# A one-layer neighbourhood-attention encoder in fp32: all second-half query, key and gate units by seven products, half of the second values inside attention, row groups in turn

## The chip, the core and the metric

The kernel runs on one core of one Trainium2 chip, as one launch. The metric is the device time of that launch in microseconds (us). Engines are named as in the profile: PE is the matrix engine (PEld its weight loads), DVE the vector engine, ACT the scalar engine, POOL the GpSimd engine, and SP the engine that issues nearly all DMAs.

## The reference

One layer on x of 2048 tokens by 1024 channels, 16 heads of 64 channels, tokens on a grid of 32 rows by 64 columns:

```python
h = rmsnorm(x, g)                       # over 1024 channels
q, k, v, gate = jnp.split(h @ w_in, 4, axis=-1)      # w_in: 1024 x 4096
# each query sees 8 rows x 16 columns of keys, plus a learned bias by relative position
s = einsum(q, k) / 8 + bias             # masked outside the neighbourhood
o = einsum(softmax(s), v)
x = x + (o * silu(gate)) @ w_out
out = rmsnorm(x, norm_f)
```

Inputs and the output are fp32, and the result is wanted at fp32 accuracy. So every large product is made of three PE matmuls: both operands are split into a high part (what the fast fp32 format holds) and the remainder, and high x high, high x low and low x high are summed in PSUM.

## The kernel before

**Tiles and units.** Weights and tokens are cut in blocks of 128 x 512. The q, k and gate columns come in units of 256 columns; there are four units of each kind, twelve in all (`units_two` names those of the second half). Tokens come in four blocks c = 0 to 3 of 512; c = 0 and 1 are the first half, c = 2 and 3 the second. One matmul of such work is 128 x 128 weights against 128 x 512, and is called a *large matmul* below. A unit over one half of the tokens takes 96 of them directly. By `seven_products`, a Strassen-like scheme with seven products of 12 matmuls on sums of blocks (weight sums S1 to S4, token sums T1 to T4), it takes 84, and adds sums and splits on DVE and ACT.

**Stages.** `stage_one` does the first half: values, then all twelve units by seven products. `stage_two` does the second half: values of tokens 8 to 15 (in tiles of 128 tokens, 24 matmuls each for one half of the heads, u = 0 or 1), then seven units by seven products. Between the value tiles, `pair` calls hand DVE and ACT the making of the token sums: `block` (normalise and split B12, B22), `t123` and `t4` (the sums), `form` and `t1` (their splits). In `seven_products`, `ahead` makes the weight sums and splits a few products early.

**Attention.** It runs in 32 *cycles*; a cycle is one pair of heads p and one group T of eight token rows. `order` sets them: T = 0 for the eight head pairs, then T = 1 and 2 for each pair in turn, then T = 3. For cycle m: scores S(m) on PE (L978); DVE adds the bias table and takes the minimum (L986); ACT exponentiates (L992); POOL divides by the sum, eight operations (L1001), in two halves of four, each after a reciprocal on DVE (L997); PE transposes T(m) (L1017), copied to SBUF by DVE and ACT (L1020); PE multiplies by the values, V(m) (L1035); DVE multiplies by the gate (L1039) and SP stores the result to DRAM (L1042).

**Filler.** PE has other work between these. The main loop issues, in its iteration m: filler, T(m-1), S(m), V(m-1). So what stands on PE between S(m) and T(m) is S(m), V(m-1) and the filler of iteration m+1. How many large matmuls the filler has is set by hand in the list `amount`. It comes first from the generator `projections` (the five units not done in `stage_two`, direct, 480 matmuls) and then from `outputs` (the output projection, 16 token tiles x 2 halves x 24 = 768 matmuls; what is left of it runs after the last cycle). The output projection of tile n reads gated results from DRAM (`load_og`, L1085, tile `ograw`), which needs the results of all eight head pairs of that row group, splits them (`split_og`, L1097 on ACT and L1098 on DVE) and multiplies (L1240 to L1244).

**What sets the order.** Each engine runs its instructions in the order in which the code issues them. `store(key, lag, f)` and `due` put an instruction off by a number of filler matmuls; `later_loads` does so for the loads of a cycle. `consume` loads and splits one filler operand (`items`: weights w, tokens x, output weights o), a few at fixed places in each cycle; `og_ready` asks whether all stores of a row group are 12 matmuls old. SP is not tied to PE: it issues until one of its DMAs has to wait.

Three lines carry the amounts:

```python
dense, end_of_it = 24.2, 24
amount = [dense] * 25
amount += [(96 * (12 - len(units_two)) + 546 - sum(amount) - first - end_of_it) / (cycles - 25)] * (cycles - 25) + [end_of_it]
```

Of the kernel before, what the change touches and what calls it, by code (L numbers as in the profile page):

```python
# [63 lines left out]
def build(ctx, tc, x, xr, xt, wg, tab, w_out, n0, nf, out):  # L64
# [90 lines left out]
    def use_item(it):  # L155
        kind, a, b = it
        state["event"] = clock[0]
        t = raws.pop(it)
        if kind == "x":
            normed("x%d1" % (a // 4 + 1), b, a % 4, t)  # L160
            split_to(hh[a, b], hl[a, b], t, None)
        elif kind == "w":
            u, ph = a
            if KINDS["v"] <= u < KINDS["g"]:
                t = t.rearrange("p (k c) -> p k c", c=256)
                a = u // 2 * 2, ph
                if u % 2 == 0:
                    wh[a, b] = wp([128, 2, 512], F32R, "wh")
                    wl[a, b] = wp([128, 2, 512], F32R, "wl")
                s = slice(u % 2 * 256, u % 2 * 256 + 256)  # L170
                h, l = wh[a, b][:, :, s], wl[a, b][:, :, s]
            else:
                w = wp([128, 2, 512], F32R, "w")
                wh[a, b], wl[a, b] = h, l = w[:, 0], w[:, 1]
            split_to(h, l, t, HD ** -0.5 if KINDS["q"] <= u < KINDS["k"] else None)
        else:
            h, l = xs([128, 512], F32R, "woh"), xs([128, 512], F32R, "wol")
            woh[a, b], wol[a, b] = h, l
            nc.scalar.activation(h, t, AF.Copy)
            nc.vector.tensor_tensor(l, t, h.bitcast(F32), OP.subtract)  # L180
# [48 lines left out]
    def units(k, j):  # L229
        return [KINDS[k] + j + i for i in range(2 if k == "v" else 1)]  # L230

    units_two = [(k, j) for j in range(2) for k in "kqg"] + [("k", 2)]
    halves = [(k, j, 1, c) for j in range(2, 4) for g in (("q", "g") if j == 2 else ("k", "qg")) for c in (2, 3) for k in g]
    attending = [False]
    last_use = {}
    for n, (k, j, ph, c) in enumerate(halves):
        for u in units(k, j):
            last_use["w", (u, ph)] = n
        last_use["x", c] = n
    end = len(halves)  # L240
    items, seen = [], set()
    for n, (k, j, ph, c) in enumerate(halves):
        a = (KINDS[k] + j, ph)
        wi = [("w", (u, ph), b) for b in range(4) for u in units(k, j)] if a not in seen else []
        xi = [("x", b, c) for b in range(4)] if c == 3 and c not in seen else []
        seen |= {a, c}
        items += xi + wi
    items += [("o", a, b) for b in range(2) for a in range(NK)]
# [7 lines left out]
    freed = set()  # L256
    state = dict(used=0, loaded=0, half=-1, done_halves=0, event=0.0)

    def may_use(it):
        kind, a, b = it  # L260
        d = state["done_halves"]
        if kind == "w":
            def tiles_(a, b):
                return (a[0] // 2 * 2, a[1], b) if KINDS["v"] <= a[0] < KINDS["g"] else (*a, b)
            live = {tiles_(*i[1:]) for i in items[:state["used"]] if i[0] == "w" and last_use["w", i[1]] >= d} - freed
            return sum(1 + (KINDS["v"] <= t[0] < KINDS["g"]) for t in live | {tiles_(a, b)}) <= 8
        if kind == "x":
            return sum(last_use["x", i] >= d for i in {i[2] for i in items[:state["used"]] if i[0] == "x"} - {b}) < 2
        if kind == "o":
            return last_use["x", 2 + b] < d  # L270
        return True
# [78 lines left out]

    def group(w, a, c, n):
        p = bank(512, "pp")
        for k in range(NK):
            if k in (1, 4, 7):
                consume(1)
            b = 2 * a + k // 4
            cols = slice(k % 4 * 128, k % 4 * 128 + 128)
            need(("w", w, b))
            need(("x", k, c))
            nc.tensor.matmul(p, wh[w, b][:, cols], hh[k, c], start=(k == 0), stop=False)  # L360
            yield 1
            nc.tensor.matmul(p, wh[w, b][:, cols], hl[k, c], start=False, stop=False)  # L362
            yield 1
            nc.tensor.matmul(p, wl[w, b][:, cols], hh[k, c], start=False, stop=(k == NK - 1))  # L364
            if k % 4 == 3 and n == last_use["w", w]:
                freed.add((*w, b))
            yield 1
        return p
# [412 lines left out]
    def stage_two():  # L781
# [3 lines left out]
        for k in range(4):  # L785
            load_x(2, "x22", k, x22[k])
        slots = {"T2": places_of([(emp, 4)] + [(kp, 2)] * 2),
                 "T3": places_of([(sp, 1)] * 2 + sixth[:5] + [(lp, 1)]),
                 "T4": places_of([(vh, 1)] * 4 + [(emp, 4)])}

        def also(n, i):
            if n == 0:
# [39 lines left out]
        def t123(*ks):  # L832
            def g():
                for k in ks:
                    a, b, c = x11[k], x12[k], x22[k]
                    nc.vector.tensor_tensor(c, c, b, OP.subtract)
                    nc.vector.tensor_tensor(b, b, a, OP.subtract)
                    nc.vector.tensor_tensor(a, a, c, OP.add)
            return g

        def t4(*ks):
            def g():
                for k in ks:
                    nc.vector.tensor_tensor(x21[k], x21[k], x11[k], OP.subtract)
# [10 lines left out]
        def t1(*ks):  # L855
            def g():
# [5 lines left out]
        pair(0, (8, 9), both(w(0, 3), lambda: spread_rstd(3)), both(lw(1, 0), block("B12", x12, 0, 1)), block("B12", x12, 2, 3),  # L862
             block("B22", x22, 0, 1))
        pair(0, (10, 11), both(v(0, 8, 9), block("B22", x22, 2, 3)), t123(0), t123(1), lw(1, 1))
        pair(0, (12, 13), v(0, 10, 11), t123(2), t123(3), both(t4(0, 1, 2, 3), lw(1, 2)))
        pair(0, (14, 15), both(v(0, 12, 13), w(1, 0)), both(w(1, 1), lw(1, 3)), w(1, 2), w(1, 3))
        pair(1, (12,), v(0, 14, 15), form("T2", x11, 0), form("T2", x11, 1))
        pair(1, (13,), both(v(1, 12), form("T2", x11, 2)), form("T2", x11, 3))
        pair(1, (14,), both(v(1, 13), form("T3", x22, 0)), form("T3", x22, 1))
        pair(1, (15,), both(v(1, 14), lambda: ahead(-9, -1)), form("T3", x22, 2), form("T3", x22, 3))  # L870
        pair(1, (8,), both(v(1, 15), lambda: ahead(-8, -1)), t1(0), t1(1), lambda: ahead(-7, -1))
        pair(1, (9,), both(v(1, 8), t1(2)), t1(3), lambda: ahead(-6, -1), form("T4", x21, 0))
        pair(1, (10,), both(v(1, 9), form("T4", x21, 1)), form("T4", x21, 2), form("T4", x21, 3))
        pair(1, (11,), both(v(1, 10), lambda: ahead(-5)), lambda: ahead(-4), both(lambda: ahead(-3), lambda: ahead(-2)),
             both(lambda: ahead(-1), v(1, 11)))
# [7 lines left out]
    def projections():  # L883
        for n, (kind, j, ph, c) in enumerate(halves):
            state["half"] = n
            w = (KINDS[kind] + j, ph)
            for a in range(2):
                if n == len(halves) - 5 and a == 0:
                    late_loads()
                    for k in range(RES_EARLY):  # L890
                        load_res(*turns_[k])
# [490 lines left out]
```

## Time and profile before

| what | value |
|---|---|
| time, median of 3 runs | 1049.65 us (1049.56 to 1051.08) |
| profiled execution, its own time | 1050.27 us |
| its span in the profile | 1048.3 us, so 2.0 us lie around the span |
| granted PE clock, mean | 0.998 |
| DVE, ACT, POOL busy | 667.6, 475.5, 215.9 us |

A matmul's record lasts longer than the distance to the next one, because matmuls are pipelined: the rate is read from how many start in a stretch, not from the mean duration. In a timeline row the first number is the start in us from the span's start, the second the length; `x32` says how many instructions of one kind are merged; the bracket gives idle time of the engine before it and what ended it. An "SPq" row is a DMA's issue, not its transfer.

### The profile page before, as it was taken

To read this page: it belongs to the slowest core of one execution; us is meant where nothing else is said; L and a number is where in the kernel's file an instruction comes from. 1 tells how busy PE (TensorE), PEld (TensorE's weight loads), DVE (VectorE), ACT (ScalarE), POOL (GpSimd) and SP (SyncE) were. 2 spreads that over 40 slices of the span, in tenths; PEclk is the share of its full clock that TensorE was granted. 3 is DMA by queue.
4 is the path that set the end of the run, shared out by engine and by line. 5 is a ranking of instruction groups with operands and counts; after the bars stand their busy time and mean duration, and the time that the engine had idled before them with its cause. 6 is when DMAs were issued, how large, how long until landed. Compare 5 with 4: busy or idle time off the path is not lost.

```text
span 1048.3 us, 19498 instructions
## 1 busy us (share of the span) xinstructions
PE 1040.0 (99%) x7084; PEld 831.7 (79%) x7084; DVE 667.6 (64%) x1542; ACT 475.5 (45%) x1164; POOL 215.9 (21%) x314
## 2 busy tenths in 40 slices
PE   9999999999999999999999999999999999999997
PEld 6888888887888888888887777777777777878786
DVE  5476657678897734565556565656677776667644
ACT  7645323234334334323226565656576655444422
POOL 0000231321321000000003333444444332313100
PEclk9999999999999999999999999999999999999999
DMA  9633444452635433333267878766987686766342
GB/s 314 228 101 107 140 149 128 132 151 98 195 120 172 120 88 94 119 92 111 91 227 263 267 252 276 231 218 218 328 269 262 227 289 210 246 229 210 107 151 81
DMA packets 112040, 191.54 MB, mean 183 GB/s; under 512 B 9864, under 2 KB 43912, under 8 KB 110920
## 3 DMA queue, kind: packets, MB, share of 16 engines
q1 hardware_dynamic: 111512, 189.90, 56.7%
q8 instruction: 56, 0.92, 0.3%
q10 hardware_dynamic: 432, 0.40, 0.1%
q14 instruction: 40, 0.33, 0.1%
HBM read 139.92 MB, written 50.33 MB: 181 GB/s over the span
## 4 chain that ended last, share of the span: by engine, by line
PE 95%; DVE 1%; issue 1%; POOL 1%; ACT 1%; DMA 0%; SPq 0%; POOLq 0%; DVEq 0%; ACTq 0%
PE pp L415 33%; PE pv L539 16%; PE o L1035 8%; PE s L978 7%; PE po L1244 5%; PE po L1242 5%; PE po L1240 5%; PE ph L1017 4%; PE pp L364 4%; PE pp L362 4%; PE pp L360 3%; POOL x L1001 1%; DMA raw<-in_wg_dram 0%; DVE f L501 0%; ACT x L992 0%
## 5 line engine op out<-in xcount | busy, mean ns | idle before, releaser
L1001 POOL TENSOR_SCALAR x<-x,st 128x360 f32<-128x360 f32 (+2 forms) x256 | 155.1, 625 | 297.4 <-DVE st L997 256.9
L415 PE MATMUL pp<-h,f 128*128 128x512 f32 x608 | 196.8, 389 | 0.0
L992 ACT ACTIVATE x<-x,st 128x360 f32<-128x360 f32 (+2 forms) x256 | 139.8, 548 | 27.3 <-DVE st L986 27.3
L415 PEld LDWEIGHTS pp<-h,f 128*128 128x128 f32 x608 | 114.1, 188 | 24.2
L415 PE MATMUL pp<-four,f 128*128 128x512 f32 x520 | 131.2, 390 | 0.1
L415 PE MATMUL pp<-l,f 128*128 128x512 f32 x304 | 118.5, 390 | 0.0
L435 POOL TENSOR_TENSOR tmp<-tmp,rb 128x512 f32<-128x512 f32 x36 | 59.3, 1648 | 269.1 <-DVE tmp L433 225.6
L415 PEld LDWEIGHTS pp<-four,f 128*128 128x128 f32 x520 | 97.5, 188 | 21.3 <-DVE u L428 0.5
L986 DVE CUSTOM_DVE_ANT_0 x<-s,em 128x360 f32<-128x360 f32 (+2 forms) x256 | 108.7, 479 | 2.0 <-PE s L978 2.0
L1020 DVE COPY pta<-ph 120x512 f32<-120x512 f32 (+5 forms) x96 | 56.0, 638 | 68.4 <-PE ph L1017 68.2
L1244 PE MATMUL po<-wol,gh 128*128 128x512 f32 x252 | 99.4, 394 | 0.0
L1242 PE MATMUL po<-woh,gl 128*128 128x512 f32 x252 | 98.7, 392 | 0.0
L1240 PE MATMUL po<-woh,gh 128*128 128x512 f32 x252 | 98.3, 390 | 0.0
L539 PE MATMUL pv<-wh,h 128*128 128x512 f32 x256 | 88.8, 392 | 0.3 <-ACT h L500 0.3
L539 PE MATMUL pv<-wl,h 128*128 128x512 f32 x256 | 88.5, 391 | 0.0
L539 PE MATMUL pv<-wh,l 128*128 128x512 f32 x256 | 88.3, 390 | 0.0
L1035 PEld LDWEIGHTS o<-pta,vt 120*64 120x64 f32 (+2 forms) x1024 | 68.5, 137 | 22.8 <-DVE st L986 15.2
L1035 PE MATMUL o<-pta,vt 120*64 120x192 f32 (+5 forms) x1024 | 83.4, 316 | 0.0
L978 PE MATMUL s<-kt,qt 64*64 64x360 f32 (+2 forms) x1024 | 80.0, 436 | 0.0
L1020 ACT ACTIVATE pta<-ph 120x512 f32<-120x512 f32 (+5 forms) x96 | 46.8, 556 | 54.0 <-PE ph L1017 54.0
L415 PEld LDWEIGHTS pp<-l,f 128*128 128x128 f32 x304 | 57.0, 188 | 12.1
L364 PE MATMUL pp<-h,w 128*128 128x512 f32 x160 | 64.2, 401 | 0.0
(162 smaller groups left out, 1642.0 us busy)
## 6 DMA issues: line engine op xcount, KB each, us to landing
raw<-in_wg_dram SPq DMA_DIRECT2D x124, 256.0 KB, 4.6
em<-in_tab_dram SPq DMA_DIRECT2D x8, 1080.0 KB, 7.9
vd<-v SPq DMA_DIRECT2D x32, 256.0 KB, 2.4
sgd<-sg SPq DMA_DIRECT2D x32, 256.0 KB, 2.5
qt<-qd SPq DMA_DIRECT2D x32, 256.0 KB, 5.4
sgt<-sgd SPq DMA_DIRECT2D x32, 256.0 KB, 6.9
ogd<-og SPq DMA_DIRECT2D x32, 256.0 KB, 2.7
xr<-in_x_dram SPq DMA_DIRECT2D x32, 256.0 KB, 4.0
```

What stands on the lines that cost most here:

```text
L364: nc.tensor.matmul(p, wl[w, b][:, cols], hh[k, c], start=False, stop=(k == NK - 1))
L415: nc.tensor.matmul(B[n, P], t[:, int(m == 2), c], x[k][int(m == 1)], start=P in (1, 6, 5) and k == 0 and m == 0, stop=k == 3 and m == 2, s ...
L539: nc.tensor.matmul(ps[t], a[:, o], b, start=k == 0 and m == 0, stop=k == NK - 1 and m == 2)
L978: nc.tensor.matmul(pst[s][h * 64:h * 64 + 64], qt[a, C * 128 + h * 64:C * 128 + h * 64 + 64], keys.rearrange("p r (s c) -> p s r c", c=8), ...
L986: nc.vector.tensor_tensor_reduce(X[i, C][s], pst[s], EM[p, ROW_TYPE[T], COL_TYPE[C], s], -1.0, 1e38, OP.add, OP.min, st[:, o:o + 1])
L992: nc.scalar.activation(X[i, C][s], X[i, C][s], AF.Exp, bias=st[:, o:o + 1], scale=-1.0, accum_out=st[:, 4 + o:5 + o])
L1001: nc.gpsimd.tensor_scalar(X[i, C][s], X[i, C][s], st[:, o:o + 1], 1.0, op0=OP.mult, op1=OP.mult)
L1020: (nc.vector.tensor_copy if h else lambda o, i_: nc.scalar.activation(o, i_, AF.Copy))(to[:k, :, 2 - j, c, h], at[h][:k, :, c])
L1035: nc.tensor.matmul(o[s * 64:s * 64 + 64, g0 * 64:g1 * 64 + 64].rearrange("d (g q) -> d g q", q=64), vt[:k, strip, s * 64:s * 64 + 64], t[: ...
L1240: nc.tensor.matmul(p, gh, woh[q, j], start=(i == 0), stop=False)
L1242: nc.tensor.matmul(p, gl, woh[q, j], start=False, stop=False)
L1244: nc.tensor.matmul(p, gh, wol[q, j], start=False, stop=(i == NK - 1))
```

## The change

- `units_two` has all twelve units. `projections` and `group` are gone; no unit of the second half is done directly.
- `stage_two` does the values of u = 0 alone (192 matmuls). Those of u = 1 for tokens 8 to 15 (192 matmuls) are the new generator `values_left`, the first filler of attention. Its weights and the reload of token block 3 stand first in `items`.
- In `stage_two` the tiles run in the order 8, 9, 12, 13, 14, 15, 10, 11; of the token sums, those of block k = 3 and all of `t4` move from DVE to POOL; the last of them are made during the first products (`then`).
- `order` takes the row groups in turn, each for all head pairs. So each cycle loads its own bias table (32 loads; before, T = 1 and 2 shared one), and row groups 0, 1, 2, 3 end with cycles 7, 15, 23, 31.
- `amount` is 18.5 for ten cycles (8 less in the first, 16 more in the second) and (192 + 546 - 193 - 16 - 24) / 22 = 22.95 after.
- `may_use` lets output weights be split once 12 and 16 value tiles are done. The first `ograw` load is no longer issued ahead by `projections`; `outputs` issues it when `og_ready` holds (or `values_left` in its last tile).

```diff
-    units_two = [(k, j) for j in range(2) for k in "kqg"] + [("k", 2)]
+    units_two = [(k, j) for j in range(4) for k in "kqg"]
+    WV = KINDS["v"] + 2, 1
+    items = [("w", (WV[0] + a, 1), b) for b in range(4) for a in range(2)]
+    items += [("x", b, 3) for b in range(4)] + [("o", a, b) for b in range(2) for a in range(NK)]
...
+        return it[0] != "o" or state["done"] >= 12 + 4 * it[2]
...
+                    e = nc.gpsimd if k == 3 else nc.vector
+                    e.tensor_tensor(c, c, b, OP.subtract)
+                    e.tensor_tensor(b, b, a, OP.subtract)
+                    e.tensor_tensor(a, a, c, OP.add)
...
-                    nc.vector.tensor_tensor(x21[k], x21[k], x11[k], OP.subtract)
+                    nc.gpsimd.tensor_tensor(x21[k], x21[k], x11[k], OP.subtract)
...
+        pair(0, (12, 13), both(v(0, 8, 9), block("B22", x22, 2, 3)), both(t123(0), t123(3)), t123(1), t123(2))
+        pair(0, (14, 15), v(0, 12, 13), form("T3", x22, 0, 1), both(form("T3", x22, 2, 3), lambda: ahead(-9, -1)),
+             form("T2", x11, 0, 1))
+        pair(0, (10, 11), both(v(0, 14, 15), form("T2", x11, 2, 3), lambda: ahead(-8, -1)), both(lambda: ahead(-7, -1), t1(0, 1)),
+             both(lambda: ahead(-6, -1), lambda: ahead(-5)), both(lambda: ahead(-4), lambda: ahead(-3), lambda: ahead(-2)))
+        ahead(-1)
+        then = [both(v(0, 10, 11), t1(2, 3)), both(t4(0, 1, 2, 3), form("T4", x21, 0)), form("T4", x21, 1, 2), form("T4", x21, 3)]
...
-    def projections():
...
+    def values_left():
+        for t in range(8, 16):
+            c, o = t // 4, slice(t % 4 * 128, t % 4 * 128 + 128)
+            p = bank(512, "pv")
...
+            for k in range(NK):
+                if t == 15 and k in (2, 4) and og_ready(k // 2 - 1):
+                    more_og()
+                for a in range(2):
+                    need(("w", (WV[0] + a, 1), k // 2))
+                need(("x", k, c))
...
+            evac_v(1, t, p)
+            state["done"] = t + 1
...
-    order = [(p, 0) for p in range(NP)] + [(p, T) for p in range(NP) for T in (1, 2)] + [(p, 3) for p in range(NP)]
+    order = [(p, T) for T in range(4) for p in range(NP)]
...
+    early, end_of_it = 18.5, 24
+    amount = [early] * 10
...
+    amount += [(192 + 546 - sum(amount) - first - end_of_it) / (cycles - 10)] * (cycles - 10) + [end_of_it]
+    fill = values_left()
...
-            if (p, ROW_TYPE[T], 0, 0) not in EM:
-                later_loads([load_tab(p, ROW_TYPE[T])], 12, 0)
+            later_loads([load_tab(p, T)], 12, 0)
```

The amounts and waits decide what stands where, so the order itself is shown at three places. The first is PE in cycle 8, the first of row group 1: the end of S(8) (`s`), V(7) (`o`), filler, and the first transposes (`ph`). Before, 24 `pp` matmuls stand between `o` and `ph`:

```order
L978 MATMUL s_6155<-kt,qt 64x360
L1035 MATMUL o<-pta,vt 64x128 x2
L1035 MATMUL o<-pta,vt 64x192 x12
L1035 MATMUL o<-pta,vt 64x128 x2
L364 MATMUL pp<-h,w 128x512
L360 MATMUL pp<-h,w 128x512
```

After, one matmul of `values_left` (its last) stands there:

```order
L923 MATMUL s_6550<-kt,qt 64x360
L980 MATMUL o<-pta,vt 64x128 x2
L980 MATMUL o<-pta,vt 64x192 x12
L980 MATMUL o<-pta,vt 64x128 x2
L843 MATMUL pv<-wh,l 128x512
L962 MATMUL ph_6640<-ident,x_6531 120x64
```

The filler of this cycle has gone from 24 to 1. Counted in the same way, with before's 24 (once 25) in each of cycles 1 to 23, the changed kernel has 19, 24, 19, 16, 15, 22 and 15 in cycles 1 to 7, 1 in cycle 8, 15 in cycle 9, 21 in cycle 10, 23 or 24 in cycles 11 to 21, 17 in cycle 22 and 22 or 23 in cycles 23 to 30 (before: 48 to 59 in cycles 24 to 30). In cycle 0 it is 50 in place of 62. After the last scores 273 output matmuls are left in place of 245.

The second place is SP around cycle 9, where the first `ograw` load (row group 0, `ogd_85`) now stands. Before, two of these loads stand together, cycles ahead of the matmuls that read them:

```order
L1042 DMA ogd_86<-og 512x1x128
L946 DMA vt<-vd_84 120x1024
L937 DMA qt<-qd_63 128x512
L153 DMA raw<-in_w_out_dram 128x512 x3
L928 DMA kt<-kd_71 128x976
L1085 DMA ograw<-ogd_85 128x1024 x2
```

After, the first stands behind the store of V(8)'s gated result (`ogd_86`, row group 1) and the load of the values of cycle 10 (`vt`):

```order
L153 DMA raw<-in_w_out_dram 128x512 x2
L871 DMA kt<-kd_69 128x976
L894 DMA sgt<-sgd_76 128x512
L987 DMA ogd_86<-og 512x1x128
L889 DMA vt<-vd_83 120x1024
L1030 DMA ograw<-ogd_85 128x1024
```

On PE, the 15 output matmuls that read it stand in the same cycle, between V(8) and the transposes T(9):

```order
L980 MATMUL o<-pta,vt 64x192 x12
L980 MATMUL o<-pta,vt 64x128 x2
L1191 MATMUL po<-woh,gh 128x512
L1193 MATMUL po<-woh,gl 128x512
L1195 MATMUL po<-wol,gh 128x512
```

The load has moved from cycles ahead to the cycle that uses it. The third place is ACT in cycle 0: the exponentials of the first half of S(0) (`x`, 264 columns), and the split of the last weight blocks of `values_left` (`wh`), which stands behind them:

```order
L937 ACTIVATE x_5068,st<-x_5068,st 128x264
L937 ACTIVATE x_5069,st<-x_5069,st 128x264
L937 ACTIVATE x_5074,st<-x_5074,st 128x264
L937 ACTIVATE x_5075,st<-x_5075,st 128x264
L443 ACTIVATE wh<-raw 128x2x256 x2
L318 ACTIVATE v<-pv 128x512
```

The eighth filler matmul after the first half of S(0) is the first that reads this `wh`, and the next reads the `wl` that DVE makes from it. Before, a token split (`h`) stood at that place, for work of a later cycle.

More of the change, by code (lines that the diff above doesn't have):

```diff
@@ L254, in now @@
         return clock[0] + 26 * runs[0]
[L256 to L257 removed]
+    state = dict(used=0, loaded=0, done=8, event=0.0)
     def may_use(it):
[L260 to L271, printed above, removed]
+        return it[0] != "o" or state["done"] >= 12 + 4 * it[2]
     def load_ahead():
```

131 lines of the change are left out of this document (32 added, 99 removed).

## The prediction

> **What bounds the kernel now.** I read the page first: its header, the PE row, the slices of PE, and the shares of the chain of waits.
>
> ```profile
> span 1048.3 us, 19498 instructions
> PE   9999999999999999999999999999999999999997
> PEclk9999999999999999999999999999999999999999
> PE 95%; DVE 1%; issue 1%; POOL 1%; ACT 1%; DMA 0%; SPq 0%; POOLq 0%; DVEq 0%; ACTq 0%
> ```
>
> PE is busy in every slice at its full granted clock, and holds 95% of the chain. A busy PE can hide short gaps here, so I read the rate from the chain in order of time:
>
> ```profile
> 94.59 147.37 PE pp L415 x648
> ...
> 328.26 84.32 PE pv L539 x372
> 412.58 133.75 PE pp L415 x588
> ```
>
> 147.37 / 648 = 0.2274, 84.32 / 372 = 0.2267 and 133.75 / 588 = 0.2275 us per large matmul, over long stretches without a break: both projection stages run at one steady rate. So does attention, as one cycle of the timeline shows (cycle 15, full width, 360 columns):
>
> ```profile
> 736.29 2.65 PE L978 MATMUL s<-kt,qt 64*64 64x360 f32 x32
> 738.88 2.61 PE L1035 MATMUL o<-pta,vt 120*64 120x128 f32 x32
> 740.67 6.41 POOL L1001 TENSOR_SCALAR x<-x,st 128x360 f32<-128x360 f32 x8 [5.84 <-DVE st L997]
> 741.41 0.50 PE L364 MATMUL pp<-h,w 128*128 128x512 f32 x1
> 742.25 0.53 SPq L1042 DMA_DIRECT2D ogd<-og  x1
> 742.51 2.18 ACT L179 ACTIVATE woh<-raw 128x512 fp32r<-128x512 f32 x4
> 742.64 0.18 DVE L997 RECIPROCAL st<-st 128x4 f32<-128x4 f32 x1 [0.42 <-ACT x L992]
> 742.88 0.58 SPq L946 DMA_DIRECT2D vt<-vd  x1
> 743.16 3.02 DVE L180 TENSOR_TENSOR wol<-raw,woh 128x512 fp32r<-128x512 f32 x4 [0.34 <-ACT woh L179]
> 743.51 0.40 SPq L937 DMA_DIRECT2D qt<-qd  x1
> 746.78 0.39 PE L362 MATMUL pp<-l,w 128*128 128x512 f32 x1
> 747.10 1.50 PE L1017 MATMUL ph<-ident,x 64*120 64x64 f32 x44
> ```
>
> Scores begin at 736.29, values at 738.88 (2.59 later), filler at 741.41 (2.53 later), transposes at 747.10, 5.69 later: 24 matmuls x 0.2275 = 5.46, and 0.23 for the two passages. So PE reaches the transposes 2.59 + 2.53 + 0.23 + 0.2275 f = 5.35 + 0.2275 f us after the scores, with f filler matmuls. Beside it runs a second path that does not depend on f: DVE, ACT, then POOL's eight products, done at 740.67 + 6.41 = 747.08, 10.79 after the scores. POOL is held up by the four DVE splits at 743.16. A cycle without such splits:
>
> ```profile
> 687.36 0.53 PE L978 MATMUL s<-kt,qt 64*64 64x360 f32 x4
> ...
> 691.74 4.52 POOL L1001 TENSOR_SCALAR x<-x,st 128x360 f32<-128x360 f32 x8 [7.30 <-DVE st L997]
> ```
>
> Here POOL is done 691.74 + 4.52 - 687.36 = 8.90 after the scores. **So PE ends every wait only as long as the filler covers 8.9 us in a quiet cycle and up to 10.8 us in one with four splits.** With f = 24 PE arrives at 10.81.
>
> **The change, part by part.** *Matmuls.* Five units leave the direct way (5 x 96 = 480) for the seven products (5 x 84 = 420); 192 value matmuls only move. 60 fewer x 0.2275 = **-13.65 us**. The sums and splits of the five units go beside products as those of the first seven do now, in the stretch of 588 that shows no break: nothing.
>
> *Entry to the products.* The token sums now have 192 value matmuls over them in place of 384. The rows of before:
>
> ```profile
> 320.28 2.38 DVE L498 TENSOR_TENSOR l<-land,h 128x512 fp32r<-128x512 f32 x2
> 320.44 1.67 POOL L435 TENSOR_TENSOR tmp<-tmp,rb 128x512 f32<-128x512 f32 x1 [10.96 <-DVE tmp L433]
> 348.67 0.68 DVE L836 TENSOR_TENSOR land<-land 128x512 f32<-128x512 f32 x1
> 358.00 1.09 ACT L372 ACTIVATE v<-pv 128x512 f32<-128x512 f32 x2 [9.00 <-PE pv L539]
> ```
>
> DVE starts the sums at 348.67; nothing ahead of that changes. Tiles 14 and 15 end before 358.00, and 48 matmuls later (10.9 us) the products begin, near 368.8. By then DVE has to do 22 operations (9 sums of tokens, 10 splits of them, 2 sums and a split of weights) of about 0.65 us, 14.3 us, and is done near 363 to 364: about 5 us early. Seven POOL operations of 1.67 us now run beside them; such a pair slows DVE from 0.69 to 1.19 us, so 11.7 us of POOL cost DVE about 5 us. The cover is just eaten, and later products ask for a split only every 12 matmuls (2.7 us). I take 0, bounds 0 and +1.
>
> *Cycle 0.* The second half of S(0) is preceded by 16 value matmuls, the eighth of which needs the `wh` behind four exponentials.
>
> ```profile
> 550.11 1.12 PE L978 MATMUL s<-kt,qt 64*64 64x264 f32 x16
> 551.16 0.50 PE L364 MATMUL pp<-h,w 128*128 128x512 f32 x1
> 553.33 0.61 ACT L497 ACTIVATE h<-raw 128x512 fp32r<-128x512 f32 x1
> ...
> L519 ACT ACTIVATE wh<-raw 128x512 fp32r<-128x512 f32 x30 | 17.4, 625 | 14.2 <-PE pv L539 10.2 <-DMA raw<-in_wg_dram 3.7 <-PE pp L415 0.2
> L522 DVE TENSOR_TENSOR wl<-raw,wh 128x512 fp32r<-128x512 f32 x30 | 19.3, 686 | 19.8 <-ACT wh L519 19.7
> ```
>
> ACT is free 553.33 - 550.11 = 3.22 after the scores; two copies of about 0.6 end at 4.4, DVE's second split at 5.1. PE would be at its eighth matmul at 1.05 + 0.11 + 7 x 0.2275 = 2.75 and at the next 0.23 later. It waits 1.65 for the first and 0.45 more for the second: **+2.1** (1.6 to 2.5).
>
> *Cycle 8.* One filler matmul stands before T(8): PE arrives 5.35 + 0.23 = 5.6 after the scores. POOL is not done then in any cycle shown, and four splits of output weights stand in this cycle as in cycle 15. There POOL's second four took 6.41 - 4.52 / 2 = 4.15, so its seventh product, which the transposes need first, is done at 10.79 - 1.04 = 9.75, and the eighth, wanted after 14 of the 44 transposes (1.50 / 44 x 14 = 0.5), holds the rest by about 0.6: a wait of 4.2 + 0.6 = 4.8. ACT has one more evacuation ahead of the splits, so they come 0.6 later: I take **+4.5**. In a quiet cycle the seventh is done at 8.90 - 0.56 = 8.34: a wait of 2.8. Bounds 2.8 to 4.9.
>
> The slowing agrees in kind with the Trainium skill, SBUF — State Buffer, section "Who interferes with whom": a DVE operation with two SBUF inputs and a GpSimd operation exclude each other for a whole instruction. By that rule four splits could add their full 3.02 us to POOL, while the rows show 6.41 - 4.52 = 1.89; by it this term would be 1.1 larger.
>
> *Cycle 9.* The first output matmuls wait for a load that is issued in the same cycle, third behind the store of the gated result.
>
> ```profile
> ograw<-ogd SPq DMA_DIRECT2D x14, 512.0 KB, 8.6
> ...
> ograw<-ogd SPq DMA_DIRECT2D x2, 448.0 KB, 5.9
> ...
> ogd<-og SPq DMA_DIRECT2D x32, 256.0 KB, 2.7
> ...
> L1098 DVE TENSOR_TENSOR gl<-ograw,gh 128x512 fp32r<-128x512 f32 x30 | 21.3, 751 | 5.8 <-ACT gh L1097 5.7
> L1097 ACT ACTIVATE gh<-ograw 128x512 fp32r<-128x512 f32 x30 | 17.1, 617 | 0.1
> ```
>
> In cycle 15 the store is issued at 742.25, the value load at 742.88, the next DMA at 743.51: 7.22 after the scores. In cycle 9 that next one is `ograw`. With its median of 8.6 to landing, 0.62 for ACT and 0.75 for DVE the first output matmuls can start 17.2 after the scores. PE is there at 2.59 + 2.53 = 5.1. **+12.1**; with the shorter landing, 5.9, 9.4; with that of a store, 2.7, 6.2. What is queued behind on PE is all of T(9) and S(10), so nothing fills the gap, and the POOL path (at most 10.8) ends inside it. The long median fits the queue: a 1.08 MB table, three 256 KB weight blocks and four cycle loads go out in the same stretch. I take 8.6.
>
> *Other cycles.* Those with 15 to 19 filler matmuls arrive at 8.8 to 9.7, behind a quiet POOL (8.3 for the seventh) but not behind one with four splits; those with 23 arrive at 10.6. Cycles 4, 10 and 22 are short of a few tenths each: **+0.6** (0 to 3). The tables, loaded in every cycle, are asked for a cycle and a half ahead, well over their landing time: 0.
>
> Sum: -13.65 + 2.1 + 4.5 + 12.1 + 0.6 = **+5.65**. Against the profiled execution (1050.27, of which 1048.3 is span) that is 1055.9. That execution is 0.6 above the median of the runs, so for a median I say **1055.3**.
>
> **The rivals.**
>
> *The load lands as fast as a store does, and POOL is quiet* (faster). 2.7 us for `ograw` gives 6.2 in cycle 9; with 2.8 in cycle 8, 1.6 in cycle 0 and nothing else the waits are 10.6, and 13.65 - 10.6 = 3.0 remain: 1046.6. It decides from a landing below about 4.5 us on, with all other terms at their low ends. For it: while PE waits, fewer other transfers are asked for. Against it: neither group of `ograw` rows is under 5.9.
>
> The Trainium skill, DMA: Bandwidth & Descriptors, section "Anatomy of one DMA", gives about 2.0 us plus bytes over 436 GB/s for one kind of DMA, which for 512 KB would be an estimate of 3.2 us and would give nearly this case; the rows of this trace, 8.6 and 5.9, differ, and I go by them.
>
> *The gain is just given back* (no change). Landing 5.9 (9.4), quiet POOL in cycle 8 (2.8), 1.6 in cycle 0: 13.8 against 13.65, so 1049.8.
>
> *Attention becomes POOL-bound in the later cycles too* (slower still). From cycle 11 to 30 each cycle has 23 or 24 filler matmuls and the DVE work of the output projection (splits of `ograw`, scalings), which ran under 48 to 59 matmuls before. Where four such operations fall beside POOL's second half, its path is 10.8 to 11 against PE's 10.6. At 0.4 in 16 cycles and 1 at the entry to the products, in place of 0.6: 12.5 slower, 1062.1. For it: DVE's two-input operations hold POOL in cycle 15. Against: they come in few cycles as many as four together.
>
> **How the numbers follow.** Forecast (waits of about 17 to 23 us, 1052 to 1059): 0.55. POOL-bound later cycles, 0.18. Just given back, 0.13. Short landing, 0.14. A run of this kernel can be told from no change by about 0.2%, 2.1 us. Slower by more: 0.55 + 0.18 = 0.73; within: 0.13; faster: 0.14. The range, 1047 to 1061, takes in the bounds of cycle 9 (6.2 to 12.1) with cycle 8 and 0 at either end, and leaves out most of the POOL-bound case and part of the fast one.
>
> **What would show it.** Right: L361 with about 1008 matmuls in the second half at the same 0.2275 and no break at its start; a PE gap of some 2 us in cycle 0, 4 to 5 us before T(8), released by POOL, and about 12 us before the first output matmul, released by DVE's split of `ograw`, with the SP row of that load about 7 us after the scores of cycle 9. The waiting time that PE shows should be near 19 us over that of before. Wrong: if `ograw` lands within 5 us, or if PE shows gaps all through cycles 11 to 30, or if the products start late.

## The result, and the profile after

The changed kernel takes **1064.47 us** (median of 4 runs, 1062.80 to 1064.92), the kernel before beside it 1050.02: a ratio of 1.0133, 95% interval 1.0116 to 1.0151. The sign was forecast, the size was not: 5.65 us slower by the sum, 14.5 measured, outside the range. The profiled execution took 1064.92, of which 1063.1 is span, 14.9 over the span before.

Two rows of the page, matmul count and slices of the granted clock:

```profile
PE 1036.2 (97%) x7024; PEld 823.3 (77%) x7024; DVE 710.6 (67%) x1595; ACT 483.3 (45%) x1175; POOL 218.8 (21%) x321
PEclk9999999999999999999999999988999999999999
```

There are 60 matmuls fewer than the 7084 before. PE still counts as busy for 97%, yet two slices of the clock, which showed a 9 in every slice before, show an 8. The waits of PE (engine, line, waited for: us in total, times, longest) say more. Before:

```profile
PE zp L117 <- DVE z L114: 1.2, 1, 1.2
PE ph L1017 <- POOL x L1001: 0.3, 1, 0.3
PE pv L539 <- ACT h L500: 0.3, 1, 0.3
```

After:

```profile
PE po L1191 <- ACT gh L1042: 8.3, 1, 8.3
PE ph L962 <- POOL x L946: 4.1, 5, 1.8
PE pv L843 <- ACT wh L443: 1.5, 1, 1.5
PE s L923 <- ACT v L318: 1.4, 1, 1.4
...
PE pv L485 <- ACT h L443: 1.2, 3, 0.4
```

The first three are the forecast's cycles 9, 8 and 0. The fourth and the last are in no step of it. All waits of the view together are 20.1 us, 18.3 more than the 1.8 before. That is near the 19 that the forecast named as a sign of being right, but 28.5 (14.9 + 13.65) have to be found: over a third of the time lost shows as no wait. The chain of waits in order of time shows that the projections are not where the rest went:

```profile
95.02 147.37 PE pp L361 x648
...
348.50 23.42 PE pv L485 x102
371.92 229.21 PE pp L361 x1008
```

229.21 / 1008 = 0.2274: one unbroken stretch at the old rate, so the products save what they should.

**An exact account.** Take the time from the first score matmul of one cycle to that of the next, less 0.2275 us for each large matmul in it, and compare with the same cycle before. Cycles 8 and 9, before and then after (window, its length, busy time of each engine, granted clock, DMA share, GB/s):

```profile
650.68:662.89 12.21, 12.21 (x136) 9.19 (x132) 7.19 (x25) 7.46 (x22) 4.82 (x8) 1.00 0.77 233
662.89:675.13 12.24, 12.24 (x137) 9.20 (x133) 7.97 (x25) 8.90 (x25) 5.35 (x8) 1.00 0.85 287
```

```profile
699.74:712.56 12.82, 9.04 (x113) 6.34 (x109) 10.19 (x28) 9.21 (x25) 6.27 (x8) 0.83 0.96 310
712.56:734.64 22.08, 13.81 (x124) 9.23 (x123) 10.01 (x28) 9.23 (x25) 4.80 (x8) 0.71 0.88 321
```

Cycle 9 before: 24 large matmuls, 12.24 - 5.46 = 6.8. After: 15, 22.08 - 3.41 = 18.7. So 11.9 are lost there. The account weighs causes of 1 to 2 us better than the medians do: in the first half, whose code is the same in the changed kernel and in every experiment, the profiles differ by up to 1.4 us. Done for every stage, by starts and counts from the trace:

| stage | forecast, us | measured, us |
|---|---|---|
| 60 matmuls fewer | -13.65 | -13.65 |
| ahead of the first scores (start, values, entry, products) | 0 (to +1) | +2.9 |
| cycle 0 | +2.1 | +5.4 |
| cycle 8 | +4.5 | +5.8 |
| cycle 9 | +12.1 | +11.9 |
| other cycles together | +0.6 (to 3) | +2.4 |
| behind the last cycle | 0 | +0.1 |
| sum | +5.65 | +14.9 |

**Half speed behind a wait.** The timeline after: the last of cycle 8's transposes, the scores of cycle 9, the request of its load and the split that follows its landing, and the first output matmuls:

```profile
710.57 2.06 PE L962 MATMUL ph<-ident,x 64*120 64x64 f32 x32 [0.80 <-POOL x L946]
712.56 3.81 PE L923 MATMUL s<-kt,qt 64*64 64x360 f32 x32
...
720.93 0.41 SPq L1030 DMA_DIRECT2D ograw<-ogd  x1
...
726.50 1.15 ACT L1042 ACTIVATE gh<-ograw 128x512 fp32r<-128x512 f32 x2 [6.47 <-DMA ograw<-ogd]
...
727.18 0.80 PE L1191 MATMUL po<-woh,gh 128*128 128x512 f32 x1 [8.27 <-ACT gh L1042]
...
729.35 0.63 PE L1193 MATMUL po<-woh,gl 128*128 128x512 f32 x1
729.78 0.63 PE L1195 MATMUL po<-wol,gh 128*128 128x512 f32 x1
```

32 score matmuls take 3.81 us where they took 2.65, and the output matmuls start 729.78 - 729.35 = 0.43 apart, not 0.2275. The windows of cycle 0 and of the same stretches (the number behind POOL's is the granted clock):

```profile
609.15:612.57 3.42, 3.42 (x12) 2.17 (x14) 0.00 (x0) 0.60 (x1) 0.00 (x0) 0.50 0.99 389
...
710.60:712.60 2.00, 2.00 (x36) 1.88 (x36) 1.41 (x3) 1.09 (x2) 0.00 (x0) 0.50 1.06 351
712.60:716.70 4.10, 4.10 (x39) 1.83 (x40) 2.89 (x10) 2.53 (x8) 0.00 (x0) 0.71 1.01 407
...
727.20:732.00 4.80, 4.80 (x11) 3.50 (x12) 3.06 (x5) 2.01 (x4) 0.00 (x0) 0.50 1.00 415
732.00:734.00 2.00, 2.00 (x32) 1.51 (x32) 0.05 (x1) 0.03 (x1) 0.00 (x0) 0.99 0.88 352
```

A PE that counts as busy all through these windows is granted half its clock, and is back at full speed from 732.0. Theory: the account is a list of separate causes, each with its own cure, and part of three of them is this half speed after idleness. The main rival is that whatever is cured comes back later, as attention is held by its other engines or by the transfers. Experiments e1 to e4 and e10 take one cause each, e5 the lack of filler, e6 to e9 all of them.

### The profile page after: what moved, and what is told of

Its sections match the earlier page's. It is cut to its first block, busy times and chain, and to the rows that moved or that the text cites. A ratio compares the mean times of both kernels' runs of the same rounds, so it can differ in the third digit from the quotient of the medians.

```text
span 1063.1 us, 19454 instructions
## 1 busy us (share of the span) xinstructions
PE 1036.2 (97%) x7024; PEld 823.3 (77%) x7024; DVE 710.6 (67%) x1595; ACT 483.3 (45%) x1175; POOL 218.8 (21%) x321
## 4 chain that ended last, share of the span: by engine, by line
PE 89%; DVE 4%; ACT 2%; DMA 2%; issue 1%; POOL 1%; SPq 1%; POOLq 0%; DVEq 0%; ACTq 0%
PE pp L361 41%; PE pv L485 10%; PE s L923 7%; PE o L980 7%; PE po L1195 6%; PE po L1191 6%; PE po L1193 6%; PE ph L962 4%; PE pv L843 3%; ACT x L937 1%; POOL x L946 1%; DVE l L444 1%; DMA sgd<-sg 1%; ACT h L443 1%; DMA ograw<-ogd 1%
## 5 line engine op out<-in xcount | busy, mean ns | idle before, releaser
L361 PE MATMUL pp<-h,f 128*128 128x512 f32 x768 | 248.5, 389 | 0.0
L361 PEld LDWEIGHTS pp<-h,f 128*128 128x128 f32 x768 | 144.2, 188 | 30.5
L361 PE MATMUL pp<-four,f 128*128 128x512 f32 x648 | 161.6, 390 | 0.1
L361 PE MATMUL pp<-l,f 128*128 128x512 f32 x384 | 149.7, 390 | 0.0
L361 PEld LDWEIGHTS pp<-four,f 128*128 128x128 f32 x648 | 121.5, 188 | 26.4 <-DVE u L374 0.5
L965 DVE COPY pta<-ph 120x512 f32<-120x512 f32 (+5 forms) x96 | 56.2, 638 | 52.9 <-PE ph L962 52.7
L923 PE MATMUL s<-kt,qt 64*64 64x360 f32 (+2 forms) x1024 | 82.1, 442 | 1.9 <-ACT v L318 1.4
L361 PEld LDWEIGHTS pp<-l,f 128*128 128x128 f32 x384 | 72.1, 188 | 15.3
L965 ACT ACTIVATE pta<-ph 120x512 f32<-120x512 f32 (+5 forms) x96 | 47.0, 557 | 65.5 <-PE ph L962 65.5
L444 DVE TENSOR_TENSOR f<-raw,f 128x512 fp32r<-128x512 f32 x80 | 55.3, 691 | 29.1 <-ACT f L443 29.1
L369 ACT ACTIVATE p<-pp 128x512 f32<-128x512 f32 x24 | 14.4, 599 | 124.3 <-PE pp L361 124.3
L485 PE MATMUL pv<-wh,h 128*128 128x512 f32 x192 | 63.9, 393 | 2.8 <-ACT h L443 1.2
L379 DVE TENSOR_TENSOR tmp<-pp,u 128x512 f32<-128x512 f32 x48 | 33.1, 690 | 47.9 <-PE pp L361 43.2
```

The costliest lines, as they stand in the source:

```text
L361: nc.tensor.matmul(B[n, P], t[:, int(m == 2), c], x[k][int(m == 1)], start=P in (1, 6, 5) and k == 0 and m == 0, stop=k == 3 and m == 2, s ...
L485: nc.tensor.matmul(ps[t], a[:, o], b, start=k == 0 and m == 0, stop=k == NK - 1 and m == 2)
L923: nc.tensor.matmul(pst[s][h * 64:h * 64 + 64], qt[a, C * 128 + h * 64:C * 128 + h * 64 + 64], keys.rearrange("p r (s c) -> p s r c", c=8), ...
L965: (nc.vector.tensor_copy if h else lambda o, i_: nc.scalar.activation(o, i_, AF.Copy))(to[:k, :, 2 - j, c, h], at[h][:k, :, c])
```

## The experiments

**e1_warm and e1b_warm: PE kept busy in cycle 9's wait** (30, then 36 matmuls of no use).

```diff
             p = bank(512, "po")
+            if k == 0:
+                for _ in range(36):
+                    nc.tensor.matmul(p, woh[0, 0][:, :128], woh[0, 0], start=True, stop=True)
```

> The changed kernel, with 30 matmuls of no use (128x512, output weights on both sides, overwritten by the first real output matmul) put in front of the first output tile, so that PE is busy in most of its 8.3 us wait for the first gated result of cycle 9. Theory A: the ten output matmuls behind that wait run 0.43 us apart, not 0.23, because the idle time halves PE's granted clock (0.50 in that stretch); with PE busy in the wait they run at 0.23 from the first, cycle 9 is 10 x 0.2 = 2.0 to 2.3 us shorter and the kernel near 1062.3. Rival B: they are slow because ACT, DVE and the transfers beside them compete for memory; then nothing changes, 1064.5, or the dummies cost something.

> As e1_warm with 36 matmuls of no use in place of 30: with 30 PE still idled 1.5 us and then 0.5 us ahead of the second real matmul, and five to six of the ten matmuls behind ran 0.43 us apart. 36 x 0.2275 = 8.2 us fill the 8.3 us wait up to its end. Theory A (idle time halves the clock): only the 0.5 us ahead of the second matmul is left of the idle time, all matmuls behind it run at 0.23, cycle 9 is 2.0 us shorter than in the changed kernel: near 1062.4. Rival B (what runs beside them slows them): they stay at 0.43 and the kernel at 1064.5.

With 30: 1061.97 us, ratio 1.0102 (1.0085 to 1.0119), but the profiled run, the slowest of the four, still shows output matmuls 0.43 us apart, and its cycle 9 is only 0.3 shorter; 1.5 us of idle time had been left. Inconclusive. With 36: 1062.14, ratio 1.0115 (1.0100 to 1.0131); in its windows the stretch behind the wait has the full clock, under the same traffic:

```profile
724.80:730.00 5.20, 5.08 (x57) 3.77 (x57) 3.38 (x6) 2.31 (x6) 0.00 (x0) 1.00 1.00 412
```

None of its output matmuls stands 0.43 from the next, and cycle 9 is 20.30 long in place of 22.08, 1.8 less. ACT, DVE and 412 GB/s of transfers beside it were much the same, so rival B falls: the idle time made them slow.

**e2_entry: the value tiles in the old order.**

```diff
-        pair(0, (12, 13), both(v(0, 8, 9), ...
-        pair(0, (14, 15), v(0, 12, 13), ...
-        pair(0, (10, 11), both(v(0, 14, 15), ...
+        pair(0, (10, 11), both(v(0, 8, 9), ...
+        pair(0, (12, 13), v(0, 10, 11), ...
+        pair(0, (14, 15), both(v(0, 12, 13), ...
```

> The changed kernel, with the value tiles before the products in the order of the kernel before (10 and 11 second, then 12 and 13, then 14 and 15; what DVE, ACT and POOL do between them unchanged). Theory A: PE's four stops between 341.9 and 348.5, about 0.56 us each, come from tiles 12 and 13 following 8 and 9 directly, so that they ask for a split block of the last tokens every 1.37 us while DVE and ACT make one in 2.05; with 10 and 11 between them the stops go and 2.3 us are gained: near 1062.2. Rival B: the block chain is just as late for whatever follows, and the time comes back as a stop at the start of the products (the sums and splits that follow end as late as now): 1064.5, with a gap of about 2 us near 359.

1062.45 us, ratio 1.0113 (1.0098 to 1.0128), and 2.25 less ahead of the first scores. By the starts of the matmuls, the 192 value matmuls take 44.0 us to the first product, 46.4 in the changed kernel (43.7 at the steady rate): 2.4 less. The products take 0.9 more, and the part before, the same code in both, happens to be 0.7 shorter. What the stops of the changed kernel were is read in its timeline:

```profile
342.94 0.74 DVE L439 SCALAR_TENSOR_TENSOR land<-land,g,rb 128x512 f32<-128x512 f32 x1
343.38 0.63 PE L485 MATMUL pv<-wh,l 128*128 128x512 f32 x2
343.71 0.63 ACT L443 ACTIVATE h<-land 128x512 fp32r<-128x512 f32 x1 [1.42 <-DVE land L439]
344.38 0.69 DVE L444 TENSOR_TENSOR l<-land,h 128x512 fp32r<-128x512 f32 x1 [0.70 <-ACT h L443]
344.39 0.30 PEld L485 LDWEIGHTS pv<-wh,h 128*128 128x128 f32 x2 [0.83 <-ACT h L443]
344.98 0.75 DVE L439 SCALAR_TENSOR_TENSOR land<-land,g,rb 128x512 f32<-128x512 f32 x1
```

One block takes 344.98 - 342.94 = 2.04 us through DVE, ACT and DVE again, and six matmuls ask for one every 6 x 0.2275 = 1.37. With two other tiles first, the blocks are ahead. Rival B holds for a part: 0.9 of the 2.4 come back in the products, and e2's list of PE's waits has one new row there, `PE pp L361 <- DVE f L444: 0.5, 1, 0.5`.

**e3_w_early: the last two value-weight splits beside the last product.**

```diff
-                if i == 5:
+                if i in (5, 6):
                     consume(2)
```

> The changed kernel, with the last two of the eight value-weight splits made beside the last product and not inside cycle 0. Theory A: cycle 0's loss begins with PE's wait for these two (1.63 + 0.58 us) and goes on with six matmuls at half the granted clock behind it (1.1 us); both go, cycle 0 is 3.3 us shorter: near 1061.2. The 1.4 us that the scores of cycle 1 wait for ACT's copy of a value tile stay. Rival B: the splits need buffers that the last product still holds, so DVE is late for the scores of cycle 0 by their 1.3 us and the wait only moves: 1063 to 1064.5.

1060.79 us, ratio 1.0097 (1.0082 to 1.0112); cycle 0 is 3.92 shorter, the wait for `wh` is gone, and of the 5.4 lost there 1.5 is left. That is the fourth row of the waits, and it stands in the timeline of the changed kernel as ACT's order:

```profile
622.98 0.63 ACT L443 ACTIVATE h<-raw 128x512 fp32r<-128x512 f32 x1 [1.42 <-DVE raw L439]
623.52 0.58 ACT L318 ACTIVATE v<-pv 128x512 f32<-128x512 f32 x1
...
624.15 2.11 PE L923 MATMUL s<-kt,qt 64*64 64x264 f32 x24 [1.38 <-ACT v L318]
```

The value tile was complete at 621.4, but its copy stands behind the fourth of four token splits, each of which waits for DVE; the scores of cycle 1 need the bank that the copy frees.

**e4_no_wo8: no output-weight splits in cycle 8.**

```diff
-                if not split_rows():
+                if not split_rows() and m != 9:
```

> The changed kernel, without the four output-weight splits of cycle 8 (they are made in cycles 10 and 11 in their place). Theory A: in cycle 8 POOL's second four products take 4.08 us, where they take 2.19 beside no such split, so T(8) gets its last operand 1.9 us earlier: cycle 8 loses 3.9 in place of 5.8, and cycle 9 is unchanged, as it waits for its load: near 1062.6. Rival B: each split shuts POOL out for its whole duration, 3.0 us in all: 1061.4. Rival C: T(8) waits for something else, or the splits cost as much in cycles 10 and 11: 1064.5.

1061.49 us, ratio 1.0110 (1.0092 to 1.0127). POOL in cycle 8, in the changed kernel and then here:

```profile
704.12 6.40 POOL L946 TENSOR_SCALAR x<-x,st 128x360 f32<-128x360 f32 x8 [6.28 <-DVE st L942]
```

```profile
704.41 4.50 POOL L946 TENSOR_SCALAR x<-x,st 128x360 f32<-128x360 f32 x8 [6.26 <-DVE st L942]
```

6.40 - 4.50 = 1.9, and cycle 8 is 1.89 shorter, as theory A has it. The median alone would speak for rival B (1061.4, where A says 1062.6); the rows decide against B's 3.0. In the profiled run, 1064.45 and again the slowest of four, cycle 9 was not unchanged but 1.1 longer. That is the half speed described above: all of its scores ran at it (4.54 us in place of 3.81), its load was requested 9.10 after the first of them in place of 8.37, and it landed 5.6 later as before.

**e10_load_early: the first load of results a cycle sooner.**

```diff
-        return all(... clock[0] - stored_at[p, T] >= 12 for p in range(NP)
+        return all(... clock[0] - stored_at[p, T] >= 4 for p in range(NP)
```

> The changed kernel, with the first load of gated results allowed 4 matmuls behind the last store of them in place of 12: it is then asked for at the end of cycle 8, one cycle earlier, and the first eight output matmuls stand in cycle 8. Theory A: PE's 8.3 us wait in cycle 9 is the time from that request to its landing (5.6 us) and the split, with nothing to fill it; it moves with the request into cycle 8, where it overlaps the wait for POOL, so that one wait is paid, not two: of 5.8 + 11.9 us in cycles 8 and 9 about 12 are left, 1058.5. Rival B: in the crowded queue the load lands at the same time whenever it is asked for, and cycle 8 gets the wait that cycle 9 had on top of its own: 1064 or more.

1067.99 us, ratio 1.0170 (1.0156 to 1.0184): worse. The time lies in rival B's range, but neither mechanism is what the timeline shows:

```profile
710.77 0.33 SPq L1030 DMA_DIRECT2D ograw<-ogd  x1
...
718.12 1.15 ACT L1042 ACTIVATE gh<-ograw 128x512 fp32r<-128x512 f32 x2 [10.35 <-DMA ograw<-ogd]
...
718.80 0.80 PE L1191 MATMUL po<-woh,gh 128*128 128x512 f32 x1 [14.28 <-ACT gh L1042]
```

The load did land a cycle sooner, which rival B denied, and the wait did move into cycle 8 and swallow POOL's, as A had it. But the request stands later in its cycle (11.9 us behind the scores; 8.4 in the changed kernel) and takes 718.12 - 710.77 = 7.35 where that took 5.6, so that cycles 8 and 9 lose 18.1 together, much as in the changed kernel (17.7); cycles 17 to 27 lose 3.9 more, which was not followed up. Asking sooner is worth nothing while PE has nothing to do meanwhile.

**e5_spread: the same filler, dealt out so that it lasts into cycle 10.**

```diff
-    early, end_of_it = 18.5, 24
-    amount = [early] * 10
+    end_of_it = 24
+    amount = [10.5, 29.5] + [13.5] * 7 + [18] * 3
...
-                if t == 15 and k in (2, 4) and og_ready(k // 2 - 1):
+                if t == 15 and k in (2, 4, 6) and ready["loaded"] < 2 and og_ready(ready["loaded"]):
```

> The changed kernel with the same filler dealt out otherwise: 13.5 matmuls a cycle in cycles 1 to 7 and 18 in cycles 8 to 10 in place of 18.5, so that the 192 value matmuls last into cycle 10 and the first gated results, whose load is still asked for in cycle 9, are wanted a cycle later. Theory A: the losses of cycles 8 and 9 (5.8 + 11.9 us over the kernel before) are the lack of filler: both go; short cycles appear in their place (cycle 6 with 8 matmuls and cycle 9 with 12, some 0.5 to 1 us each; cycles 4 and 5 with four splits and 13 matmuls, about 1.3 each; cycle 10 with three weight splits and four of results, 1 to 2): 17.7 - 5 = 12.7 gained, near 1052. Rival B: the load of the results is late whenever it is asked for, or the tables of 1.08 MB, now asked for every 9 us, are: cycle 10 waits 5 to 8 us and the kernel is at 1057 to 1060.

1056.75 us, ratio 1.0062 (1.0048 to 1.0076). Cycle 8 loses nothing now and cycle 9 0.6, and 7.7 us come back, more than half of the loss. With the filler the request moved too: the last value tile now makes it, at 706.5, 18 us before the first output matmul. As e10 shows that an earlier request alone gains nothing, the lack of filler was the cause. The price elsewhere was under-estimated, 10 by the medians in place of 5: 3.1 in cycle 10, 6.2 in cycles 4 to 7. There the list of PE's waits puts two down to transfers, though not to those that rival B named (the load of the results and the tables):

```profile
PE ph L962 <- POOL x L946: 2.0, 4, 1.0
...
PE s L923 <- DMA ogd<-og: 1.4, 1, 1.4
PE s L923 <- DMA kt<-kd: 1.4, 1, 1.4
PE po L1191 <- ACT gh L1042: 1.2, 1, 1.2
```

**e6_all, e7_even, e8_even_b, e9_best: all cures together.** e6 joins e2, e3 and e5's request of the load with filler of 14 a cycle (19 in cycles 8 and 9, 21 in 10) and at most two weight splits a cycle.

> All cures together: values in the old order ahead of the products (e2), value-weight splits done ahead of attention (e3), 14 matmuls a cycle in cycles 1 to 7, 19 in 8 and 9 and 21 in 10 with less give and take between cycles, and at most two output-weight splits in a cycle. Theory A: the account is additive and nothing else is lost with the change: 13.65 us of matmuls less, and of the 28.5 us of new waits 2.3 (entry), 3.9 (cycle 0), 17.7 (cycles 8 and 9) and most of the 2.4 of the other cycles go: 1064.5 - 26 = 1038 to 1041, ratio 0.989 to 0.992. Rival B: with less filler the cycles 1 to 10 are bound by the softmax path or by transfers (two or three tenths each, 1 to 2 us in those with splits): 1045 to 1050.

1049.55 us, ratio 0.9994 (0.9985 to 1.0004): no different from the kernel before that can be measured, and A's sum failed by some 10. The time is in rival B's range, but cycles 2 to 9 lose 1.2 together, so B's mechanism is a small part of it. PE's waits name what was new:

```profile
PE s L923 <- ACT v L318: 2.3, 1, 2.3
PE po L1191 <- ACT gh L1042: 2.2, 1, 2.2
PE s L923 <- DVE pta L965: 1.5, 3, 0.6
```

The first is the value copy of e3 again; with less filler PE meets it sooner. The second is the split of the first results, made only when the output matmuls ask for it; it also put DVE's split ahead of the reciprocals, so that POOL's second half began 2.35 late. Behind both waits the clock was at half for 3.4 us, so cycles 1 and 10 lose 1.8 and 4.3. The third were put down to output tiles that end just ahead of the scores. e7 takes these on (and e8 with slightly other amounts):

```diff
-    ready = dict(loaded=0, split=0, res=RES_EARLY)
+    ready = dict(loaded=0, split=0, res=RES_EARLY, turn=0)
...
-                    consume(1 + (m == 1 and k < 3), turn=True)
+                    consume(int(k == 0) if m <= 4 else k % 2, turn=True)
...
+    amount = [10.5, 29.5] + [13] * 7 + [15] * 2
+    amount += [24] * (cycles - len(amount)) + [end_of_it]
-    calm_debt = 6
+    calm_debt = 1
```

> As e6_all, with what was left there taken on: the first gated results are split in cycle 10 as soon as they are there, behind 14 value matmuls, and not by the first output matmul that asks for them; the four last token blocks are normalised and split one a cycle in cycles 0 to 3, not four in cycle 0; and every cycle from 11 on has exactly 24 filler matmuls, so that an output tile never ends just ahead of the scores. Theory A: in e6_all the waits left over the kernel before are 13.15 us, of them 4.3 in cycle 10, 4.2 in cycles 0 and 1 and 3.2 in cycles 25 to 30; these go but for some 0.5 each, and 13 matmuls in the narrow cycles with two splits cost 0.3 each: 3 to 5 us of waits against 13.65 gained, 1039 to 1042, ratio 0.990 to 0.992. Rival B: with 13 to 15 matmuls a cycle the path over DVE, ACT and POOL sets each of the ten first cycles, or the tables do: 1045 and more.

> As e7_even with 13.5 matmuls in cycles 1 to 7 and a give and take of 2 matmuls between cycles in place of 1 (an output tile ends 11 matmuls into a cycle). Theory A of e7_even: within 1 us of it. If the phase at which the output tiles end matters by itself, it differs by 2 us or more.

e7: 1044.71, ratio 0.9952 (0.9939 to 0.9966). e8: 1049.28, ratio 0.9985 (0.9974 to 0.9997). e7 is 2.7 above its forecast; its cycles 1 to 7 lose 0.4 to 0.8 each, 3.8 together, as rival B's mechanism would have it. e8 is not within 1 us of e7 but 4.6 above it (3.4 in the profiles), the sign that its expectation named for the phase at which the output tiles end: it loses 0.9 to 1.6 us each in cycles 18, 20, 22, 26, 28 and 30, e7 so much in cycle 26 alone and 0.6 in cycle 18, and its list of waits has the row `PE s L923 <- DVE pta L965: 4.7, 7, 1.2`, which e7's has not. e8 has half a matmul more in cycles 1 to 7 as well, so the phase is the likely cause and not shown alone. e9 moves seven matmuls from cycle 0 to cycles 1 to 7 (`[10.5, 22.5] + [14] * 7 + [15] * 2`) and asks for a row tile's scalings sooner (a lag of 4 in place of 9).

> As e7_even, with seven value matmuls moved out of cycle 0 (its transposes stood ready 1.7 us) into cycles 1 to 7, which get 14 each, and the two scalings of a finished row tile asked for 5 matmuls sooner, so that they no longer stand on DVE just ahead of the copies before the scores (cycles 18 and 26 lost 0.6 and 1.5 by that). Theory A: cycles 1 to 7 lose 0.2 less each (1.4), cycles 18 and 26 2.0 less in all: 1044.7 - 3.4 = 1041.3, ratio 0.992. Rival B: the path over DVE, ACT and POOL in cycles 1 to 7, not PE, is what is 0.4 to 0.8 too long, and PE with one matmul more arrives no later than it: cycles 1 to 7 unchanged in length, so they gain the same 0.2275 a matmul; but the scalings meet POOL's second half in their new place: 1043 to 1045.

1042.61 us beside 1049.81, ratio 0.9930 (0.9917 to 0.9944): faster than both kernels, between theory A's time and rival B's. The seven matmuls paid: cycles 1 to 7 take 68.2 us with them, 68.7 in e7 without, so PE did not set their length, as rival B has it; the scalings did not help cycles 18 and 26 (1.1 and 1.5 lost, 0.6 and 1.5 in e7). What PE waits for now:

```profile
PE zp L117 <- DVE z L114: 1.2, 1, 1.2
PE s L923 <- ACT pta L965: 0.9, 3, 0.3
PE pv L485 <- ACT h L446: 0.6, 1, 0.6
PE pp L361 <- DVE f L444: 0.5, 1, 0.5
PE ph L962 <- POOL x L946: 0.2, 1, 0.2
```

Of 28.5 us of new loss 5.7 are left (its span, 1040.3, is 8.0 under that before: 13.65 - 8.0).

## Why the forecast was wrong, step by step

- **Matmuls, -13.65: right.** 60 fewer, one stretch of 1008 at 0.2274 without a break.
- **Entry, 0: the step that failed outright.** The working held that nothing changes ahead of DVE's sums and asked only whether DVE is done before the products begin. So it was: no wait stands there in the changed kernel. It did not ask which tile asks for which block on the way. Tiles 12 and 13 ask every 1.37 us for blocks that come every 2.04. Of the 2.9, some 2.6 lie in these value matmuls, and e2's order takes 2.4 off them; 0.4 is the part before, which differs from profile to profile.
- **Cycle 0, +2.1: right as a wait, short as a cost.** The waits for `wh` and `wl` were 1.5 and 0.3. With the half speed behind them they cost 3.9 (e3). 1.5 more is ACT's order in the same cycle: the working of this cycle has no term for the four token splits that stand ahead of a copy that frees a bank.
- **Cycle 8, +4.5: right, and short by the clock.** The waits for POOL are 4.1 together, five pauses of at most 1.8 as its products come one by one (forecast: two, of 4.2 and 0.6). The last transposes begin 10.8 after the scores, as the forecast's terms have it (9.75 + 0.5 + 0.6). The remaining 1.7 is transposes at half speed and their short pauses. e4's 1.89 is the difference that the rows of cycle 15 gave. By the exclusive rule of the Trainium skill, SBUF — State Buffer, section "Who interferes with whom", as the prediction read it, the splits could have added 3.0. The trace does not agree: 1.9 was measured.
- **Cycle 9, +12.1 against 11.9: right by two errors.** The load took 726.50 - 720.93 = 5.6 to land, not 8.6, so that the first output matmul came 14.6 after the scores and not 17.2. In return the scores ran at half speed (+1.2, and the request at 8.4 in place of 7.2; in e4 the scores took 0.7 more and the request came 0.7 later) and so did ten output matmuls (2.0; 1.8 by e1b). The choice of the long median was wrong; the mechanism, a load asked for and wanted in one cycle, was right.
- **Other cycles, +0.6: within the bounds, short.** 2.4, most of it in cycles 1 to 5. What each of these waits for was not followed up.
- **Rivals.** Short landing did come (5.6), but not below the 4.5 from which it would have decided, and with dearer waits. Cycles 11 to 30 did not become POOL-bound: most of them lose 0.0. That this rival's time, 1062.1, is the nearest to the measured one is luck.

In short, each place was found but one, and the waits were priced as if PE resumed at full speed. Entry (2.9), the clock (about 5.6: 1.6 in cycle 0 by e2 and e1b, where it stayed at full, 1.0 in T(8), 1.2 and 1.8 in cycle 9), the bank (1.5) and the other cycles (1.8) are, less 3 by the landing, 8.8 of the miss of 9.3. The 1.6 and the 1.8 rest on profiles with and without the half speed, the 1.0 and the 1.2 only on the lengths of its rows.

## What to carry to other kernels

Work that is moved to fill gaps must last until the next work can start, load and split included: list for every cycle what PE has to do, and for every first use when its load was asked for; a cycle whose filler runs out costs a whole latency. A wait of some microseconds on PE is dearer than its length, as matmuls behind it can run at half clock. And an in-order engine is a queue: ask not only whether it is done in time, but what stands ahead of the one copy that frees a bank.

## What was not expected of the hardware

The granted clock fell to 0.5 after quite short idle times. In cycle 0 PE idled 1.5 and 0.3 us; then the clock was half from 609.15 to 612.57, 3.4 us. Of the seven profiles that have this same wait, three show matmuls 0.43 apart behind it and four do not (e2, e1b, e10 and e5, cycle 0 shorter by 1.55 in the first three). So the same code costs 1.6 more or less. The traces say what tells the three from the four. In each, every change of the granted clock lies a multiple of 3.41 us (3413 ns) from every other, which marks off stretches of that length. In the three profiles the two idle times fall into one such stretch, in the four an edge falls between them, or (e10) into the second. Here the stretch with the idle times in the changed kernel, which the row of cycle 0 above follows, then the two of e2 (columns as above):

```profile
605.74:609.15 3.41, 1.62 (x7) 0.81 (x6) 1.32 (x4) 2.15 (x8) 0.00 (x0) 1.00 1.10 165
```

```profile
602.45:605.86 3.41, 1.94 (x8) 1.29 (x8) 1.77 (x10) 3.15 (x10) 0.00 (x0) 1.00 1.14 213
605.86:609.27 3.41, 3.10 (x22) 1.96 (x25) 0.59 (x1) 0.60 (x1) 0.00 (x0) 1.00 0.96 342
```

PE is busy for 1.62 to 1.64 us of the stretch in the three, and for at least 1.89 of each in the four. So the phase of the wait goes with the outcome in all seven, though no run set it on purpose, and busy time alone is not the rule: in e5 a stretch with 1.67 busy (618.26 to 621.67) was followed by the full clock, in e1_warm one with 1.87 (725.51 to 728.92) by half. The Trainium skill, TensorE: Matmul & The Clock Gate, Part 1, describes half rate after an idle window of about 3.4 us that runs free of the kernel; the half rate and the 3.4 us agree with these rows, and that less idle time is enough does not.
